# A hybrid decoder step: 44 instead of 60 adaLN weight pieces inside of the recurrence

## The chip, the cores and the metric

The kernel runs on one core of a Trainium2 chip. The metric is the device time of one execution in microseconds, the median of several runs. Beside the runs there is one profiled execution, from which all rows below come.

## The reference, cut to what matters

A trunk of two layers is computed for a prompt of 256 rows and for 8 single rows (264 columns in all), with d_model 2048 and d_ff 5632. Layer 0 mixes with RWKV-7, layer 1 with an RG-LRU; behind each mixer stands a ConvFFN. Each of the four blocks has its own shift, scale and gate, and they come from the condition `c` by one wide product for each layer:

```python
mod = (jax.nn.silu(c) @ P['w_mod'][i] + P['b_mod'][i]).reshape(B, N_MOD, 1, D_MODEL)
sh_m, sc_m, gt_m, sh_f, sc_f, gt_f = [mod[:, j] for j in range(N_MOD)]
h = rms_norm(x, P['norm_g'][i, 0]) * (1 + sc_m) + sh_m
...
out, shift_new, S = rwkv7_time_mix(...)
...
x = x + gt_m * rms_norm(out, P['norm_g'][i, 1])
```

So of the 12 vectors of `mod` the first two are needed at once, and the other ten only as the blocks are reached: the gate of the mixer behind the recurrence, the shift and scale of the first ConvFFN after that, and so on. `w_mod` is 2048 x 12288 for each layer in f32. The recurrence of RWKV-7 is, per head and step, S = S * d + (S a) b + v k and y = S r; the kernel works it out in chunks of 64 steps, for 16 pairs of heads.

## The kernel before

The program has four stages for layer 0: the projections (weights streamed in groups, each a matmul of three for hi and lo parts), the recurrence over 16 pairs of heads, the output projection, and the ConvFFN; then layer 1 with RG-LRU and ConvFFN. Everywhere but in the recurrence TensorE multiplies streamed weights: `Stream` (`ws`) loads raw tiles of 1 MB, two groups in each, ScalarE and VectorE split each group into `wh` (L434) and `wl` (L435), and 24 matmuls of 264 columns (L455 to L457) use it.

The ten later vectors of `mod` are cut into 160 pieces of 1 MB (`in_wmr`), 16 for each vector. A piece is loaded into a raw tile and used by 4 matmuls of 512 columns in `wm_mm` (L345); after 16 of them VectorE transposes the sum (L394) and `mod_fin` finishes the vector. There are two places for it:

- Inside of the recurrence, by `pump_load` (a step that issues the first half of the load, and a step for the second, L1397) and `pump_step` (the matmuls). The first `NPUMP` pieces go there.
- Behind it, by `mm_group`, which calls `wm_pump(1)` after every `PACE`-th group of weights; that uses the piece loaded before and loads the next (L375). `residual_and_h` puts in four more at each of three seams, and `mod(layer, vec)` forces in what a vector still lacks when it is asked for.

Raw tiles go around in a ring of `NRAW + stg["n"]`, five outside of the recurrence, where weights and pieces share it. In the recurrence `stg["n"]` is 0 and only the `NRAW` resident tiles `raw` are left, for pieces and four loads of the sample's low-rank weights:

```python
def raw_tile():
    i = stg["i"]
    stg["i"] = (i + 1) % (NRAW + stg["n"])
    return rawp([128, 2048], F32, "raw", NRAW) if i < NRAW else stg["p"](..., "rawx", stg["n"])
```

A tile that comes around again may be loaded only when its last reader is done, and the load's issue waits for that on SyncE, in order with all other transfers of the recurrence.

What runs when in the recurrence is written out by hand in the string `ORDER`. Each entry is a letter and a number, with a count ahead of it: `l` load, `p` prep, `d` diag, `s` solve, `v` levels, `b` prepb, `q` seq, `o` out (for the pair with that number), `a` a piece of the sample's state, `g`, `h`, `e` the sample's preparation, gate and end, `w` a step of the load of a piece, `u` its matmuls. Each entry runs its job to its next `yield`, and the instructions so issued are put on each engine in that order: a table that sets all five engines' queues.

Of the kernel before, what the change touches and what calls it, by code (L numbers as in the profile page):

```python
# [38 lines left out]
l3 w1 p2 d0 3p2 4p1 a1 2b0 d1 b0 2b1 3g0 3p2 b1 p2 l5 p2 3p3 l3 2p3 2b0 d0 d1 s0 p3 w1 2p3 u0 u1 2p2 s2 3p3
5b1 p4 p3 2l4 g0 2p4 p5 s0 2p5 p4 3g0 l5 p5 w2 s0 w2 w3 2g0 p2 w3 g0 l6 p2 d2 p3 g0 5p2 6p3 d3 u2 u3 2g0 s0  # L40
3p4 2b2 w4 p4 3p5 b2 b1 4p4 b1 2p5 2b2 g0 s0 3b2 d2 d3 w4 2s2 5g0 p5 w5 3g0 2p4 u4 3p4 l7 p4 3b3 p5 2s2 s0 p5
2b3 g0 2b2 w5 u5 3b3 g0 p5 2w6 2p5 p4 2p5 p6 q0 2p6 2a0 2p5 u6 2a0 2q0 l6 s0 v0 b3 p6 2a0 5p6 b3 p6 s2 a0 p6
a0 3v0 2p7 a0 4h0 l8 l9 p7 l7 p7 d5 d4 l8 w7 2h0 3p7 4p8 v1 p7 v1 h0 2v1 l9 2p7 2v0 h0 p7 2p9 h0 p9 v1 s2 v1
p9 3v0 2v1 v0 v1 d4 d5 v1 2a1 p7 v0 q0 p6 w7 u7 2w8 u8 3s4 2a1 3q0 s2 2v2 q0 v1 w10 v2 3q0 p7 a1 p7 3q0 p7 2w9
v2 p6 l10 2q0 2p6 q0 2p6 s4 q0 2p6 a1 3p7 v3 3q0 v3 a0 s4 2a1 w10 v2 2p8 q0 2o0 q0 v3 v2 3b4 p8 a1 u9 u10 a1
p7 2p8 d6 3p8 l10 a2 p10 v3 o0 3p10 b5 o0 a2 q1 v3 2q1 d7 q1 2w11 o0 d6 q1 v3 s4 2a2 v2 d7 s4 v2 a2 a3 v2 w12
q0 2o0 s6 2p8 d8 2q1 v2 2o0 p8 a2 s4 3q1 o0 v2 p8 p9 s6 q1 l12 2q1 2a2 d8 q1 v3 q1 2p8 2a2 2p9 v3 4o0 3v3 3v4
q1 v4 3b4 a3 a2 b4 p8 b4 p9 3a3 w12 u11 u12 p9 v4 b4 3q1 2v4 a4 v4 b4 4q1 3a3 v4 h0 2s6 2w13 3p9 2b5 2p10 2b5
p10 2w14 b6 a3 2l11 3b5 a3 2v4 p10 p11 q1 a4 u13 u14 a3 2w15 b5 2o1 2w16 s6 a5 b5 3p9 p10 2q2 2a4 p9 q2 p9 d9
v5 2o1 a4 o1 2p11 2p9 o1 2v5 o1 s6 p11 s6 2q2 o1 u15 3q2 2w17 a4 2o1 a4 b7 d9 s8 3q2 2v5 a4 v5 2q2 a4 3q2 u16  # L50
4q2 s6 2w18 v5 q2 b6 p11 2q2 2p11 3v5 p11 3o2 3v6 3p10 v5 o1 b6 2p12 u17 u18 q3 p12 q3 a4 l12 p12 v6 a5 3p10
2q3 2l13 2b6 q3 o1 a4 q3 2b6 2w19 v6 2o2 w20 v6 s8 q3 a5 q3 p10 2q3 b6 q2 2o2 2p10 a5 w20 2a5 3v6 a6 u19 u20
p10 l14 o2 4q3 4a5 d10 2o2 w21 4q3 2v6 a5 2b6 q3 w21 2q3 p12 b7 q3 2p12 b7 o3 o2 o3 q4 s8 u21 d10 2o1 w22 2o2
w22 w23 u22 q4 q3 4p11 3q4 o2 p11 2a6 2q4 3p11 b8 4q4 2p11 2v7 w23 u23 2w24 2v7 d11 p13 2v7 a7 3p13 q3 p11 2q4
u24 2w25 w26 5q4 p12 w26 3v7 4s8 3q4 2a6 d11 2o3 l14 2q4 o4 p12 2v7 o3 u25 2o4 p12 2q5 2p12 q4 3a6 p12 2q5 w27
s10 w27 2a6 p12 d12 2p12 2b8 s14 a7 3p13 p12 a7 s8 4p14 2o3 q5 o3 o4 p13 u26 u27 q5 2p12 o4 v8 2l15 2o3 3v8 o3
d12 3q5 2b7 a7 2b7 3q5 2b8 q5 2a7 b8 4q5 b7 2w28 u28 o4 2p14 w29 b7 o3 q5 2o4 a7 b7 v8 b8 w29 o4 v8 o4 u29 3b8
v8 2q5 o4 a6 2a7 2w30 2v8 2s10 2o3 q5 v8 2q5 p13 v9 o5 2w31 a7 3p13 u30 a8 a7 u31 v8 o5 o4 5b9 a8 q6 a8 q5
2p13 3q6 a8 q6 2p13 2s10 b10 s10 p13 2b9 3a8 2w32 u32 q6 p15 2p14 p15 p14 p15 2w33 3o5 q6 p15 2w34 s10 d13 2q6
2o4 q6 u33 q6 w35 2q6 w35 b9 a8 v9 3q6 v9 2p13 v9 q6 2a8 2b9 q6 d13 2q6 v9 o5 2q6 p15 v9 o6 2p15 q6 a9 p15 o6  # L60
u34 u35 q7 o5 a8 p14 q7 2o5 2w36 w37 2p14 3q7 2o5 s10 p14 a9 p14 d14 p14 w37 4q7 v9 u36 w38 2v9 3a9 q7 p15 2v9
2a9 4q7 2b10 3q7 s12 4b10 w38 4q7 s12 2p14 3a9 2q7 a9 v10 u37 u38 a10 v11 2s12 v10 2p15 s12 p15 b11 p15 2v10
2p15 2w39 2p15 a11 4b11 v10 2b11 2v11 v10 2a10 3v10 v11 q6 q7 u39 2o6 s12 2o7 q8 d15 v10 4q8 v10 2w40 u40 2w41
2q8 a10 o5 s12 2o6 a10 2o6 o5 u41 5q8 w42 o5 w42 o6 2q8 o6 q8 o7 o6 o7 q8 u42 o7 p14 w43 q8 a10 2q8 a10 w43
3a10 v11 3q8 o8 q8 w44 o6 w44 o8 q9 v11 2o6 o7 4q9 2o8 2o7 q9 2a11 p14 a11 q9 u43 u44 d14 d15 o7 s12 v12 2q9
w45 o7 q9 w45 o8 2w46 o8 v12 4q9 3o8 2q9 o7 u45 3q9 v12 2w47 v12 o8 2v12 4q9 2o9 2s14 q10 o7 a11 2o7 o9 q10
s14 2q10 a10 q8 q10 2o9 b10 u46 2o8 3o9 2w48 u47 q10 b10 o9 q10 o9 b10 2q10 2b12 2q10 b12 3b11 4o9 o8 u48 2q10
b12 2q10 o8 q10 2b12 2w49 q9 b12 2a11 b12 2a11 q10 b13 3q10 2w50 b13 2q10 2s14 q10 2b12 2o10 u49 u50 a12 o10
q10 2o10 6b13 2a11 b14 w51 2b14 w51 4b14 a12 o10 u51 4o10 v13 2w53 2b13 3v11 3v12 a12 b14 3a12 v13 2p15 2v13
a12 2v11 v12 w52 v13 w52 q11 v13 u52 u53 2q11 v12 3a12 3q11 2a13 2b14 q11 v13 q11 s14 q11 v13 b15 q11 s14 q11  # L70
2v14 v13 a12 2o10 v14 w54 v14 v13 4a13 v14 w54 a13 v13 v14 w55 q11 w55 q11 u54 5q11 o10 3a13 q11 a13 2q11 b15
2q11 o10 2o11 q12 u55 2o11 q12 b15 2q12 o11 b15 v15 2q12 b15 2q12 2a14 b15 q12 2b15 a14 q12 2o11 2v15 4q12 v15
2o11 2w56 a14 q12 o11 3q12 q11 2v15 2a14 2q12 2b15 2q12 2o12 a14 q13 2q12 u56 2o11 2o12 o11 a14 2o12 o11 3q13
3o12 2q13 w57 o12 2a14 2q13 3o12 2q13 v14 2q13 o12 v14 2q13 v15 v14 q13 w59 2v15 2v14 a15 q13 4a15 2q13 2a15
w57 u57 3q13 a15 3q13 2o13 q14 v15 3q14 a15 v15 5q14 a15 3q14 o13 e0 o13 a15 10q14 o14 e0 o14 q14 4q15 o13
4q15 w58 6q15 o14 q15 e0 q15 w58 6q15 u58 e0 2o13 q15 2e0 q14 o14 o15 o14 e0 w59 u59 o15 2o13 2o14 4o13 o14
o13 6o14 a14 q15
# [1714 lines left out]
```

## Time and profile before

| | us |
|---|---|
| median of 3 runs | 2910.57 |
| lowest, highest | 2909.17, 2916.7 |
| profiled execution | 2907.63 |
| its span | 2905.9 |
| TensorE busy (matmul) | 2786.0, 96% |
| VectorE, ScalarE, GpSimd busy | 1756.3, 1366.6, 511.6 |

The span runs from the first to the last instruction. The recurrence is the stretch from 397 to 772 us: its first matmul on L969 starts at 397.51, and the first matmul of the output projection at 770.86.

### The profile page before, as it was taken

Reading aid. Unit: us, or ns where it says so; the run is one execution under the profiler, and the core shown is the slowest. Engines: PE = TensorE matmul, PEld = TensorE weight load, DVE = VectorE, ACT = ScalarE, POOL = GpSimd, SP = SyncE. Lnnn points to the kernel's source line nnn. Section 1 sums busy time; section 2 is a strip of 40 time slices with the busy share of each in tenths; the row PEclk is TensorE's granted clock in tenths of the full one; section 3 lists DMA queues with packets and bytes.
Section 4 is the critical chain, followed back from the end, with each engine's and each line's share of the span. In section 5 each row is a group of like instructions: output and inputs, shape, how many; then the busy total and the mean of one; then the engine's idle time right before and its main releaser. Section 6 shows DMA issues by size and latency. Waiting matters only on the chain.

```text
span 2905.9 us, 61725 instructions
## 1 busy us (share of the span) xinstructions
PE 2786.0 (96%) x25868; PEld 2529.8 (87%) x25868; DVE 1756.3 (60%) x2830; ACT 1366.6 (47%) x2195; POOL 511.6 (18%) x1044
## 2 busy tenths in 40 slices
PE   7999988989899999999999999999999999999997
...
DMA  8777557887565666666666665566666645545452
GB/s 329 285 264 257 171 162 230 286 269 250 209 248 214 234 242 229 235 234 231 233 235 229 242 258 188 220 231 221 261 221 236 231 176 181 182 177 186 174 188 77
DMA packets 148438, 648.48 MB, mean 223 GB/s; under 512 B 41360, under 2 KB 60960, under 8 KB 81600
## 3 DMA queue, kind: packets, MB, share of 16 engines
...
q14 instruction: 76, 0.62, 0.1%
...
## 4 chain that ended last, share of the span: by engine, by line
PE 74%; DMA 4%; DVE 3%; ACT 2%; issue 1%; SPq 0%; POOL 0%; DVEq 0%; ACTq 0%; POOLq 0%
PE bk L455 16%; PE bk L456 15%; PE bk L457 15%; PE sq L455 6%; PE sq L456 6%; PE sq L457 6%; PE wm L345 5%; DMA raw<-in_wmr 3%; PE bk L895 1%; DVE bt L545 1%; ACT wh L434 0%; PE bk L901 0%; DVE U L546 0%; PE bk L582 0%; PE bk L1231 0%
## 5 line engine op out<-in xcount | busy, mean ns | idle before, releaser
L435 DVE TENSOR_TENSOR wl<-rawx,wh 128x1024 fp32r<-128x1024 f32 x460 | 565.4, 1231 | 488.2 <-ACT wh L434 468.5
L434 ACT CAST wh<-rawx 128x1024 fp32r<-128x1024 f32 x460 | 481.1, 1048 | 663.2 <-PE bk L456 454.2
L455 PE MATMUL bk<-AH,wh 128*128 128x264 f32 x2352 | 672.7, 286 | 0.0
L457 PE MATMUL bk<-AH,wl 128*128 128x264 f32 x2352 | 668.7, 284 | 0.2 <-DVE wl L435 0.2
L456 PE MATMUL bk<-AL,wh 128*128 128x264 f32 x2352 | 668.8, 284 | 0.0
L435 DVE TENSOR_TENSOR wl<-raw,wh 128x1024 fp32r<-128x1024 f32 x300 | 369.3, 1233 | 329.8 <-ACT wh L434 323.3
L455 PE MATMUL bk<-ah,wh 128*128 128x264 f32 x1822 | 525.7, 289 | 8.0 <-ACT ah L488 5.5
L457 PE MATMUL bk<-ah,wl 128*128 128x264 f32 x1822 | 520.8, 286 | 0.5 <-DVE wl L435 0.5
L456 PE MATMUL bk<-al,wh 128*128 128x264 f32 x1822 | 520.8, 286 | 0.0
L434 ACT CAST wh<-raw 128x1024 fp32r<-128x1024 f32 x300 | 313.7, 1048 | 434.8 <-PE bk L456 285.0
L455 PEld LDWEIGHTS bk<-AH,wh 128*128 128x128 f32 x2352 | 443.4, 189 | 34.4 <-issue 29.3
L456 PEld LDWEIGHTS bk<-AL,wh 128*128 128x128 f32 x2352 | 442.7, 188 | 0.2 <-DVE AL L489 0.2
L457 PEld LDWEIGHTS bk<-AH,wl 128*128 128x128 f32 x2352 | 441.8, 188 | 0.4 <-DVE wl L435 0.4
L455 PEld LDWEIGHTS bk<-ah,wh 128*128 128x128 f32 x1822 | 344.2, 189 | 33.9 <-issue 21.6
L457 PEld LDWEIGHTS bk<-ah,wl 128*128 128x128 f32 x1822 | 344.6, 189 | 1.4 <-DVE wl L435 0.8
L456 PEld LDWEIGHTS bk<-al,wh 128*128 128x128 f32 x1822 | 344.7, 189 | 0.6 <-DVE al L489 0.2
L455 PE MATMUL sq<-AH,wh 128*128 128x264 f32 x1040 | 297.3, 286 | 0.0
L456 PE MATMUL sq<-AL,wh 128*128 128x264 f32 x1040 | 295.7, 284 | 0.0
L457 PE MATMUL sq<-AH,wl 128*128 128x264 f32 x1040 | 295.4, 284 | 0.0
L1525 POOL COPY fgs<-gt 128x10 f32<-128x10 f32 x88 | 49.4, 585 | 1306.8 <-ACT gt L1519 1285.6
L455 PEld LDWEIGHTS sq<-AH,wh 128*128 128x128 f32 x1040 | 196.0, 189 | 15.2 <-issue 13.4
L456 PEld LDWEIGHTS sq<-AL,wh 128*128 128x128 f32 x1040 | 195.7, 188 | 0.0
...
## 6 DMA issues: line engine op xcount, KB each, us to landing
...
```

Source lines behind the costliest of these rows:

```text
L345: PE.matmul(ps[32 * g:32 * g + 32, :cols], cs[:, k0 + kk, :], raw[:, (kk * 4 + g) * cols:(kk * 4 + g + 1) * cols], start=(k0 + kk == 0), s ...
L434: S.copy(wh, t)
L435: V.tensor_sub(wl, t, wh.bitcast(F32))
L455: PE.matmul(ps[:, :n], h[:, kk, sl], xh, start=first and kk == 0, stop=False)
L456: PE.matmul(ps[:, :n], h[:, kk, sl], xl, start=False, stop=False)
L457: PE.matmul(ps[:, :n], l[:, kk, sl], xh, start=False, stop=last and kk == 1)
L545: e.tensor_tensor(t, U1[:, j:j + n, :TP], r1[:, None, :TP].to_broadcast([128, n, TP]), op=mult)
L895: PE.matmul(out[HH[(i + turn) % 2]], lhs[HH[i]], rhs[HH[i]], start=start, stop=stop, skip_group_check=True)
L1525: G.tensor_copy(gs[:, m], gt[:, TP:])
```

## The change

`NPUMP` falls from 60 to 44, so 116 instead of 100 pieces go behind the recurrence. `NRAW` rises from 2 to 3: three resident tiles go around in the recurrence, and outside the ring of five is three resident and two others. `PACE` falls from 5 to 4, so a piece goes with every fourth group of weights. `ORDER` is written anew; it holds the same steps of all other jobs. No function changes.

```diff
-PACE = 5
-NRAW = 2
+PACE = 4
+NRAW = 3
 CW = (3, 1)
-NPUMP = 60
+NPUMP = 44
...
 ORDER = """
-p0 s0 h0 g0 l0 p0 l0 3p0 g0 3p0 2l1 4p1 4p0 2g0 4p1 g0 3p1 p0 p1 b0 a0 4p0 l2 2p0 p2 b0 l2 2b0 2p1 w0 p1 b0 w0
...
+p0 p1 2g0 2l0 2p0 l1 p1 p0 s0 l1 p0 g0 3p0 l2 4p0 p1 l3 2p0 2w0 5p1 2p0 4p1 p2 3p0 p2 2g0 p3 p2 l2 p2 3p1 3b0
...
```

SyncE in the middle of the recurrence, before: `raw` from `in_wmr` is half a piece, `ss` and `sS` the sample's state; PE in the bracket is a wait for a matmul, the DMAHW names are waits for earlier transfers.

```order
L1397 DMA raw_7923<-in_wmr 128x1024 [waits DMAHW1_49,PE_49]
L1397 DMA raw_7923<-in_wmr 128x1024
L1397 DMA raw_7938<-in_wmr 128x1024 [waits PE_49]
L1397 DMA raw_7938<-in_wmr 128x1024 [waits DMAHW4_49]
L1358 DMA out_sS<-ss_7229 128x512 [waits DMAHW5_49]
L1397 DMA raw_8032<-in_wmr 128x1024 [waits DMAHW2_49,DMAHW6_49,DMAHW1_49,PE_49]
L1397 DMA raw_8032<-in_wmr 128x1024 [waits DMAHW7_49]
L1397 DMA raw_8079<-in_wmr 128x1024 [waits DMAHW3_49,DMAHW4_49,DMAHW0_49,PE_49]
L1397 DMA raw_8079<-in_wmr 128x1024
L1335 DMA ss_8093<-in_swkv 128x512 [waits DMAHW5_49]
L1358 DMA out_sS<-ss_7504 128x512 [waits DVE_49]
```

The same place now (`vj`, `kj` are a pair's values and keys, `lu2` its gate weights):

```order
L1396 DMA raw_7952<-in_wmr 128x1024 [waits DMAHW5_49,PE_49]
L1396 DMA raw_7952<-in_wmr 128x1024 [waits DMAHW6_49]
L1396 DMA raw_7989<-in_wmr 128x1024 [waits DMAHW7_49,PE_49]
L1396 DMA raw_7989<-in_wmr 128x1024 [waits DMAHW0_49]
L1334 DMA ss_8013<-in_swkv 128x512 [waits DMAHW1_49,DVE_49]
L1029 DMA vj_8075<-Vd_97 128x256 [waits DMAHW2_49,DVE_49]
L1396 DMA raw_8101<-in_wmr 128x1024 [waits DMAHW3_49,PE_49]
L1396 DMA raw_8101<-in_wmr 128x1024 [waits DMAHW4_49]
L956 DMA kj_8108<-Kd_96 128x256 [waits DMAHW5_49,Pool_49]
L1196 DMA lu2_8126<-in_lup 128x256 [waits DMAHW6_49,PE_49]
L1396 DMA raw_8160<-in_wmr 128x1024 [waits DMAHW7_49]
L1396 DMA raw_8160<-in_wmr 128x1024 [waits DMAHW0_49]
```

Before, five rows of pieces are broken by one other transfer and each piece's first row waits for a matmul; now two other transfers stand between them twice, and the last piece's first row waits for none.

SyncE at the end of the recurrence, before: `pS` is a pair's final state, `in_wst` the weights of the output projection.

```order
L1397 DMA raw_10582<-in_wmr 128x1024 [waits DMAHW6_49,DMAHW3_49,PE_49]
L1197 DMA lu2_10606<-in_lup 128x256 [waits DMAHW4_49]
L1397 DMA raw_10582<-in_wmr 128x1024
L1186 DMA out_pS<-St_10526 64x64 [waits DVE_49]
L1186 DMA out_pS<-St_10526 64x64 [waits DMAHW7_49]
L1397 DMA raw_10367<-in_wmr 128x1024 [waits DMAHW0_49]
L1358 DMA out_sS<-ss_10071 128x512 [waits DMAHW1_49]
L1186 DMA out_pS<-St_10627 64x64 [waits DMAHW2_49,DVE_49]
L1186 DMA out_pS<-St_10627 64x64 [waits DMAHW3_49]
L1197 DMA lu2_10728<-in_lup 128x256 [waits DMAHW4_49,PE_49]
L420 DMA raw_10753<-in_wst 128x2048 [waits DMAHW5_49]
L420 DMA raw_10755<-in_wst 128x2048 [waits DMAHW6_49,DMAHW0_49]
```

And now:

```order
L1258 DMA so2_10495<-sd2_5759 128x1x128
L1396 DMA raw_10462<-in_wmr 128x1024 [waits DMAHW3_49]
L1396 DMA raw_9971<-in_wmr 128x1024 [waits DMAHW4_49]
L1396 DMA raw_9674<-in_wmr 128x1024 [waits DMAHW5_49]
L1185 DMA out_pS<-St_10512 64x64 [waits DMAHW6_49,DVE_49]
L1185 DMA out_pS<-St_10512 64x64 [waits DMAHW7_49]
L1185 DMA out_pS<-St_10378 64x64 [waits DMAHW0_49]
L1185 DMA out_pS<-St_10378 64x64 [waits DMAHW1_49]
L1357 DMA out_sS<-ss_10016 128x512 [waits DMAHW2_49]
L1357 DMA out_sS<-ss_9824 128x512 [waits DMAHW3_49]
L1196 DMA lu2_10610<-in_lup 128x256 [waits DMAHW4_49,PE_49]
L419 DMA raw_10635<-in_wst 128x2048 [waits DMAHW5_49]
```

The last halves of the pieces moved ahead of the last two pairs' state transfers, where one stood behind them; the first weights follow the last `lu2` in both.

TensorE at the end of the recurrence, before: `yb` is the last state step's output, `wm` the pieces; the other rows are `pair_out` of the last pairs and the sample's transpose (`sy`).

```order
L895 MATMUL yb_10547<-E_10050,rb_10626 64x64 x2
L345 MATMUL wm_9408<-raw_10582,cT_72 32x512 x4
L1210 MATMUL bk_10648<-blk_108,gsq_10493 128x2 x2
L1390 MATMUL bk_10657<-ident_107,sy_5460 128x128
L1202 MATMUL bk_10663<-yh_10539,cen_113 128x256
L1203 MATMUL bk_10663<-yl_10540,cen_113 128x256
L345 MATMUL wm_9408<-raw_10367,cT_72 32x512 x4
L1219 MATMUL bk_10648<-ident_107,gsd_10651 64x128 x4
L1210 MATMUL bk_10683<-blk_108,gsq_10662 128x2 x2
L1231 MATMUL bk_10691<-lw_98,lu2_10485 128x256 x2
L1219 MATMUL bk_10683<-ident_107,gsd_10686 64x128 x4
```

And now:

```order
L1209 MATMUL bk_10526<-blk_108,gsq_10393 128x2 x2
L1201 MATMUL bk_10532<-yh_10404,cen_113 128x256
L1202 MATMUL bk_10532<-yl_10405,cen_113 128x256
L344 MATMUL wm_8646<-raw_10462,cT_72 32x512 x4
L344 MATMUL wm_8646<-raw_9971,cT_72 32x512 x4
L344 MATMUL wm_8646<-raw_9674,cT_72 32x512 x4
L1209 MATMUL bk_10557<-blk_108,gsq_10531 128x2 x2
L1218 MATMUL bk_10526<-ident_107,gsd_10555 64x128 x4
L1230 MATMUL bk_10571<-lw_98,lu2_10246 128x256 x2
L1218 MATMUL bk_10557<-ident_107,gsd_10565 64x128 x4
L1230 MATMUL bk_10582<-lw_98,lu2_10411 128x256 x2
```

Two pieces, four rows apart, became three in one row, behind the first norm matmuls of the last pairs instead of ahead of them.

## Rows read from the trace of the kernel before

**Rows 1.** The slices of the page: TensorE and the DMA engines.
```profile
PE   7999988989899999999999999999999999999997
...
DMA  8777557887565666666666665566666645545452
```

**Rows 2.** Busy time by stage: recurrence in three stretches and whole, then behind it.
```profile
core 0: us, PE busy (x) PEld busy (x) DVE busy (x) ACT busy (x) POOL busy (x), PEclk, DMA share, GB/s
397.00:547.00 150.00, 123.93 (x2271) 79.38 (x2270) 106.54 (x257) 78.96 (x189) 74.08 (x175) 0.94 0.81 250
547.00:697.00 150.00, 133.03 (x2405) 79.28 (x2397) 82.46 (x186) 62.32 (x173) 64.48 (x163) 0.98 0.85 271
697.00:772.00 75.00, 62.48 (x1241) 41.70 (x1239) 42.08 (x103) 30.72 (x93) 11.44 (x14) 0.80 0.52 174
397.00:772.00 375.00, 319.44 (x5900) 200.35 (x5898) 231.08 (x545) 172.00 (x455) 149.99 (x351) 0.93 0.77 244
1000.00:1050.00 50.00, 50.00 (x409) 46.63 (x402) 26.88 (x36) 20.77 (x28) 3.13 (x12) 1.00 0.62 229
2400.00:2450.00 50.00, 50.00 (x413) 50.00 (x413) 28.02 (x39) 22.32 (x30) 4.17 (x12) 1.00 0.48 179
```

**Rows 3.** The same view, adaLN pieces (L345) alone, over the recurrence.
```profile
core 0: us, PE busy (x) PEld busy (x), PEclk, DMA share, GB/s
397.00:772.00 375.00, 94.42 (x480) 14.52 (x480) 0.93 0.77 244
```

**Rows 4.** Waits over the recurrence: in total, times, longest (us).
```profile
PE wm L345 <- DMA raw<-in_wmr: 24.4, 20, 4.3
...
PEld wm L345 <- DMA raw<-in_wmr: 54.5, 40, 5.2
```

**Rows 5.** The waits of TensorE, middle stretch, 547 to 697 us.
```profile
PE wm L345 <- DMA raw<-in_wmr: 15.7, 15, 4.3
```

**Rows 6.** Chain of work over the recurrence: shares by line, and one long piece.
```profile
by line: DMA raw<-in_wmr 24.8%; PE wm L345 12.1%; PE bk L895 6.1%; PE bk L901 3.7%; issue 3.5%; PE bk L1231 2.3%; PE bk L1219 2.2%; PE sq L895 2.1%; PE bk L914 2.0%; PE yb L895 1.9%; DMA xc<-sx 1.6%; PE bk L1210 1.5%; DMA ss<-in_swkv 1.5%; 
...
637.57 8.88 DMA raw<-in_wmr
```

**Rows 7.** TensorE in order of time: a split piece, later a whole one.
```profile
551.04 1.05 PE L345 MATMUL wm<-raw,cT 128*32 128x512 f32 x4
553.61 1.05 PE L345 MATMUL wm<-raw,cT 128*32 128x512 f32 x4 [1.52 <-DMA raw<-in_wmr]
...
726.28 1.07 PE L345 MATMUL wm<-raw,cT 128*32 128x512 f32 x8
```

**Rows 8.** SyncE in order of time, middle stretch: loads and the next transfer.
```profile
548.15 6.88 SPq L1397 DMA_DIRECT2D raw<-in_wmr  x3
555.08 0.43 SPq L1030 DMA_DIRECT2D vj<-Vd  x1
```

**Rows 9.** TensorE in order of time, the recurrence's last two pieces.
```profile
754.98 1.93 PE L345 MATMUL wm<-raw,cT 128*32 128x512 f32 x8
...
758.53 1.94 PE L345 MATMUL wm<-raw,cT 128*32 128x512 f32 x8
```

**Rows 10.** TensorE in order of time, first ConvFFN: two pieces.
```profile
983.64 1.06 PE L345 MATMUL wm<-rawx,cT 128*32 128x512 f32 x8
...
999.43 1.07 PE L345 MATMUL wm<-raw,cT 128*32 128x512 f32 x8
```

**Rows 11.** Chain of work, seam before the second ConvFFN (start, us, what).
```profile
2076.03 2.71 PE wm L345 x24
```

More of the change, by code (lines that the diff above doesn't have):

```diff
@@ L37 @@
 ORDER = """
-p0 s0 h0 g0 l0 p0 l0 3p0 g0 3p0 2l1 4p1 4p0 2g0 4p1 g0 3p1 p0 p1 b0 a0 4p0 l2 2p0 p2 b0 l2 2b0 2p1 w0 p1 b0 w0
[L39 to L77, printed above, removed]
+p0 p1 2g0 2l0 2p0 l1 p1 p0 s0 l1 p0 g0 3p0 l2 4p0 p1 l3 2p0 2w0 5p1 2p0 4p1 p2 3p0 p2 2g0 p3 p2 l2 p2 3p1 3b0
@@ new lines @@
+p2 b1 p2 b0 2w1 b0 3p2 4p1 g0 b0 l3 l4 d1 p3 p2 l4 d0 b0 p2 2p3 2b1 w2 3b0 u0 w2 2p3 2p2 2p3 p4 p3 5p2 3p3 2p4
+a0 d0 g0 d1 p4 2g0 b2 p2 u1 3b1 2s0 p3 h0 p3 2g0 d2 2l5 2p3 u2 d3 b1 p5 2w3 s0 d2 g0 s0 4g0 w4 g0 2s0 d3 2p4
+2b1 2p3 b1 2p4 4b2 s2 p4 l6 p4 p3 2g0 2p4 w5 2p5 s2 4p5 3g0 4p4 b3 2p4 g0 2p5 u3 3p5 2g0 3b2 b3 p5 2b3 s0 p5
+g0 p5 b3 2p5 v0 3p6 2v0 w4 2v0 u4 l6 v1 q0 g0 p6 s2 2g0 a0 l7 p4 v0 p5 w6 v1 p5 s2 3a0 2s2 l7 2p6 a0 p6 2q0
+3p7 b2 2v1 w5 u5 2p7 b2 2p6 w6 u6 v0 p6 p7 2p6 2v1 2v0 2b3 2v0 4a0 b3 3h0 2b3 l8 b4 4p7 l8 h0 s2 p8 p7 s4 d5
@@ new lines @@
+2p8 h0 2q0 v1 d4 p8 q0 p9 v1 q0 l9 w7 s2 v2 3p7 4h0 2q0 3v1 q0 d4 3q0 l9 2q0 2p9 a1 p7 d5 2q0 p7 s6 p7 p9 6p6
+2p7 2q0 a1 2q0 b5 3v2 2q0 d7 2o0 l10 w8 b4 p6 v3 b4 q1 p8 l11 2v2 2q1 w8 q1 v3 2s4 3p8 2v2 v3 a1 w7 s4 q1 2p8
+v2 u7 o0 2s4 q1 v3 3q1 v2 q1 d6 2p8 q1 p9 w10 a0 v2 v3 o0 v3 a1 2w9 w10 2a1 2p9 3q1 s4 q1 3a1 2p8 l10 2q1 d6
+d7 3o0 s6 q1 o0 a1 u8 u9 2p10 p9 p8 2o0 2p10 3a2 u10 2b4 2a2 b4 a1 3q1 s4 v4 v3 b4 2v3 3a2 2q1 v5 p9 3v4 2v3
+2p8 3b5 2b4 2b5 p8 2p9 a2 p9 w12 2o0 v4 b5 b4 2w11 w12 b5 u11 u12 v4 s6 2b5 o0 2o1 l11 6q2 v4 q0 2w13 u13 o0
@@ new lines @@
+2v4 2a2 p8 s6 2v5 o1 3a3 2w15 2v4 w14 p9 v5 3q2 2p9 2q2 a3 2p9 a3 d8 p9 2s6 3q2 p10 p11 q2 w14 2o1 2p11 p10
+2q2 p9 q2 2v5 2p10 w16 2a3 3q2 o1 s10 d8 q2 s6 2a3 p11 q2 o2 2o1 u14 u15 o1 o2 p10 w16 2p10 q3 p10 v5 3q3 o2
+u16 2v5 a4 v5 p12 o1 v5 s6 v6 b6 2o2 q1 v6 d9 2q3 p11 a3 q3 2a4 b6 a3 p10 3q3 l12 v6 w17 a4 q2 2a4 v6 b6 q3 a4
+2b6 3q3 w17 4p10 a4 o1 b6 q3 v6 2b6 p10 l12 3q3 v6 q3 p11 s8 q3 b6 2q3 o3 2a4 o3 a5 q3 a5 w18 p10 w18 b6 2p12
+2o2 u17 b7 o2 l13 3q4 b7 p11 3p12 d9 2q4 w19 u18 b7 w19 d10 2o2 5p11 2w20 l13 a5 4q4 2v6 3v7 p12 v7 v6 a5 o2
@@ new lines @@
+q4 a4 2s8 p12 2p11 v6 o1 2q4 u19 v6 p12 2o1 o2 s8 2w21 d11 2q4 2p11 a6 3q4 2v7 2p11 w22 p11 q4 w22 3q4 p13 3a5
+p13 2o2 p13 2q4 u20 2l14 2p13 u21 o3 p13 o3 2p12 o4 v7 2p12 o4 o3 q5 a5 o4 p14 2a5 2s8 v7 a6 2v7 2w23 q3 s8
+2p12 4q5 p13 v7 p12 p14 p12 w24 3a6 o3 a6 2p14 a6 w24 3q5 o4 u22 u23 2q5 2o3 q5 2o3 s8 3o4 2q5 b8 3q5 v8 o3
+2b7 2o4 b7 q5 o4 q5 v8 2p12 2b7 a6 q5 2v8 a5 2b8 q5 b8 a6 o3 q5 d10 q4 l15 2p13 3b8 2b7 2v8 2q5 u24 d11 s10
+3b8 2w25 2o5 v8 q6 2w26 2s10 2q6 a6 2a7 v8 u25 v8 2q6 v9 2p14 p13 2v8 a7 3q6 2a7 o4 b9 2o3 q6 a7 2b9 a7 3q6
@@ new lines @@
+2w27 2o4 l15 u26 o4 p13 u27 s10 3o5 p15 2b9 3p13 w28 q6 w28 w29 2q6 s10 3p13 w29 a7 3q6 a6 b9 s10 q6 q5 q6 2b9
+q6 p14 3v9 2q6 3p15 b9 2o5 w30 u28 2p13 b9 3o6 u29 q7 v9 b10 q7 2o5 w30 p14 o5 s14 v9 b10 2a7 b10 3p14 d12 3q7
+3v9 o6 s12 u30 v9 a8 p14 p15 s10 2q7 v9 2q7 p15 o6 p14 p15 q7 2b10 2a8 w31 v10 w31 3q7 2p14 q7 d13 b10 2q7 v10
+2a8 2q7 u31 2w32 q7 p14 2v10 b10 2q7 3a8 2p15 a7 q7 2o7 q7 a8 q8 p14 2v10 q6 u32 4q8 v10 2o5 v11 q8 v10 2o5
+2v10 d12 d13 s12 2w33 q7 v10 q8 p15 a8 p15 2q8 b11 p15 5b11 q8 o6 a8 b11 2o7 3q8 3a9 q8 u33 3o6 2w34 q8 p14 o7
```

13 lines of the change are left out of this document (added).

## The prediction

> **What bounds the kernel now.** I read the slices of the page first, to find where TensorE is not the limit, then the busy time of each stage, then the waits inside of the one stage that has some, and last the chain of work through it.
>
> The slices [rows 1] show a TensorE at 9 tenths or more almost everywhere, with 8s among them in slices 6 to 11 of 40: that is the recurrence, and in slices 7 to 10 the DMA engines are at 7 or 8 tenths, more than anywhere later. By stage [rows 2]: the recurrence lies from 397 to 772 us, 375 us long. TensorE is busy for 319.4 of them and idle for 55.6. Behind it TensorE has no idle time at all: 50.00 of 50 us. So time saved in the recurrence is time saved, and work put behind it costs its full length.
>
> What the adaLN pieces do in the recurrence is in [rows 3]. A piece is 8 rows of the trace (4 matmuls, each shown twice), and 480 rows are 60 pieces. They are busy for 94.4 us, 1.57 each, though a piece whose data is there takes 1.07 from start to end, some 1.0 beside its neighbours [rows 7]. The difference is the wait: each half of a piece has its own load, and where the second half is late, the piece falls apart into two runs of 1.05 us with a hole of 1.52 between them [rows 7]. TensorE's idle time before such halves is 24.4 us in 20 waits, most of it in the wait of 15.7 us that the middle stretch shows; its weight loads wait for the same transfers another 54.5 us, partly under a matmul that still runs [rows 4, 5]. The chain of work says the same: the loads of pieces are the largest part of it, 24.8% of the 375 us, one of them 8.88 us [rows 6].
>
> Why they are late: two tiles hold the pieces, so a load starts only when the piece two before it is done, and SyncE stands at that load with all other transfers queued behind it (three loads in a row take it 6.88 us [rows 8]). The transfers themselves have room: 244 GB/s over the stage against 271 in its middle stretch [rows 2].
>
> **The change, part by part.** The sum is made against the profiled execution, 2907.6 us with a span of 2905.9; it lies 2.9 under the median of the runs, 2910.6.
>
> 1. 16 pieces leave the recurrence. In flow 1.0 us each: -16.0.
>
> 2. The third tile. A load may now start when the piece three before it is done, and pieces stand further apart (44 in the stage for 60). Two terms can shrink: the stretch of the pieces, 94.4 - 60 x 1.0 = 34.4 us, and the idle time, 24.4 us. Bounds: nothing of it goes, or all 58.8. I take two thirds per piece, since a free issue takes SyncE 0.43 us and three loads took 6.88 [rows 8]: most of that delay is the wait to be issued, which a third tile takes away, while a load issued in time still needs some us to land. What is left: (34.4 + 24.4) / 3 x 44 / 60 = 14.4. Gain: -44.4.
>
> 3. What is late next. In the middle stretch TensorE's idle time is 16.97 us, and 15.7 of it are these loads: only 1.3 us in 150 go to other engines. The two other stretches idle 26.07 and 12.52, of which at most 24.4 - 15.7 = 8.7 are loads: about 30 us in 225, or 0.133 per us, go to VectorE, ScalarE and small transfers [rows 2, 4, 5]. With the loads out of the way the middle stretch will wait for those as the others do: bounds 0 and the whole gain of parts 1 and 2, 60 us; I take the rate of the nearest stretches, 0.133 x 115 = +15.
>
> 4. The new order of the steps. Its parts are the same instructions, so it has a price only in waits, which part 3 has. Two places can be read from the rows of the order. In the middle, SyncE had four pieces' loads with one other transfer among them, each first half waiting for TensorE; now two pieces, two other transfers, a piece, two others and a piece follow each other, and the last one's first half waits for no matmul any more. At the end, TensorE had one piece right behind the last state step and one four rows later; now three stand in a row. A piece there takes 1.93 us, with a granted clock of 0.80 in that stretch (part of it at the lower of the two levels, 1.2 GHz) [rows 2, 9]: one more is +1.9. Their loads stand ahead of the last two pairs' state transfers on SyncE, so I don't charge a wait; if one came it would cost at most a load as long as the longest, 8.88 [rows 6]. The first weights behind the recurrence are queued behind the last gate load in both versions: 0.
>
> So the recurrence goes from 375 to 375 - 16.0 - 44.4 + 15 + 1.9 = 331.5 us.
>
> 5. The pieces that come back later. 116 instead of 100 are left, and one goes with every fourth group of weights instead of every fifth. Counting groups (24 in the first output projection, 256 in a ConvFFN, 56 and 32 in the RG-LRU) pieces go 6 for 4, 64 for 52, 14 for 11 and 8 for 6: 19 more inside of full TensorE. By then 144 pieces are done, as many as the second ConvFFN's scale needs; before it was 141, and three pieces were forced in at that seam. Price in full TensorE: two pieces are 15.79 us apart [rows 10]; five groups without a piece take 5 x 24 x 50 / 413 = 14.53 [rows 2]; a piece is 1.26. 19 x 1.26 = +23.9. The seam gives back the three pieces that the chain shows there, 2.71 [rows 11]. Net +21.2. The transfers have room for it: three tiles of 1.05 MB, two of weights and a piece, in 4 x 2.906 + 1.26 = 12.9 us are 244 GB/s, under the 271 of [rows 2], so 0 for them; bound from above, if each of the 116 waited for its load as the 60 do now, 24.4 / 60 x 116 = 47, of which I take nothing, since the 50 us with pieces of [rows 2] have no idle time.
>
> Sum: -16.0 - 44.4 + 15 + 1.9 + 21.2 = -22.3. 2907.6 - 22.3 = 2885.3; against the median 2888.3. I say **2888**.
>
> **A rule that speaks against the change.** The weight loads are busy for 200.35 of 375 us in the recurrence, 53%, and for 46.6 of 50 behind it [rows 2]. The Trainium skill (Perfetto Trace Analysis, Identifying the Most-Contended Engine) says to judge TensorE's headroom by the busy share of its weight loads and not of its matmuls, and (Optimization Strategy) that stages with different most-contended engines may gain by being interleaved. By that rule the recurrence has the free room for pieces, and moving them behind it puts them where there is none: parts 1 and 2 would be nothing and the sum +23. Against it, in this trace, stand the 24.4 us in which TensorE waits for pieces and nothing else, so I follow the rows and keep the rule's outcome as the third rival.
>
> **Rivals.**
>
> First, all of the waiting goes. Parts 1 and 2 in full are -16 - 58.8 = -74.8, part 3 is 0: -74.8 + 1.9 + 21.2 = -51.7, or 2859. For it: only 1.3 us of other idle time in the middle stretch. Against it: VectorE is busy for 106.5 of 150 us in the first one, which a faster TensorE makes denser.
>
> Second, the wait stays with each piece: the third tile doesn't help, because SyncE still comes to the load late, behind a transfer whose data isn't ready. Then 16 pieces take their share along, 16.0 + 16 x 58.8 / 60 = 31.7; part 3 shrinks in proportion to 15 x 32 / 60 = 8. Sum -31.7 + 8 + 1.9 + 21.2 = -0.6: 2910, no change. That is also what a change that doesn't do what it says would give: fewer pieces, no third tile in effect.
>
> Third, slower: the recurrence doesn't wait for loads at bottom but for the chain of small dependent steps (state update, copy, matmul), and each load that arrives earlier uncovers one of these. Its place is the middle stretch, its price that parts 1 to 3 cancel: 1.9 + 21.2 = +23, 2934. It decides from the point where the recurrence shortens by less than 21.2 - 8.7 = 12.5 us. For it: of the 38.6 us of idle time outside of the middle stretch at most 8.7 are loads. Against it: in the middle one 15.7 of 16.97 are.
>
> **Chances.** The measurement tells a change from none at about 0.3%, 8.7 us: 2902 to 2919 counts as the same. The forecast (2871 to 2902) 0.53, the first rival (under 2871) 0.20, the second 0.14, the third 0.13. Faster is the forecast and the first rival, 0.73; same 0.14; slower 0.13. For eight in ten I leave out the slower case and the far end of the first rival (more than all of the waiting gone, by an order that packs better): 2853 to 2909.
>
> **What would show it.** Part 1 and 2: a recurrence of about 330 us with 352 rows of pieces, busy for under 60 us, and TensorE's idle time for their loads at some 6 us for 24.4. Part 3: more waits for VectorE and ScalarE in the middle. Part 4: three pieces in a row at the end, 1.9 us each, without a hole. Part 5: pieces 12.9 us apart behind the recurrence, TensorE still full, and no three pieces at the seam near 2076 us; everything from the first output projection on 21 us longer. Wrong I am if the recurrence keeps more than 360 us, if its idle time moves to other releasers in the same size, or if a piece in full TensorE costs much more than 1.26 us.

## The result, and the profile after

The changed kernel takes 2886.47 us (median of 4 runs, 2882.78 to 2888.66) against 2910.88 for the kernel before on the same chip: a ratio of 0.9911, with an interval of 0.9894 to 0.9929. It is faster by 24.4 us; 2888 was forecast. Its profiled execution is 2882.8 us with a span of 2881.0, 24.9 under the span of before.

Where it came from can be read from three ends. The first matmul of the recurrence's decay (L968, L969 before) starts at 399.93 us, 2.4 later than before; the first matmul of the output projection at 726.25, 44.6 earlier; and from there to the end of the span it is 2154.8 us for 2135.0. So the recurrence itself went from 373.35 to 326.32 us (-47.0), and the stages behind it became 19.7 us longer. 2.4 - 47.0 + 19.7 = -24.9.

The view of [rows 2], busy time by stage, of the changed kernel (the columns are the stretch, its length, each engine's busy time and instructions, then the granted clock, the DMA engines' share and GB/s):

```profile
397.00:547.00 150.00, 121.78 (x2284) 82.40 (x2285) 108.15 (x256) 79.82 (x194) 67.28 (x167) 0.91 0.79 244
547.00:672.00 125.00, 118.50 (x2561) 82.07 (x2561) 89.34 (x198) 65.43 (x185) 75.82 (x173) 1.00 0.80 251
397.00:727.00 330.00, 286.29 (x5772) 196.95 (x5771) 231.82 (x541) 169.98 (x455) 152.21 (x351) 0.93 0.73 228
1000.00:1050.00 50.00, 50.00 (x404) 46.07 (x403) 23.25 (x29) 21.56 (x30) 2.09 (x6) 1.00 0.69 252
```

The last row is the first ConvFFN: as full as before, though a piece comes with every fourth group now. In the recurrence, the middle stretch has 6.5 us of idle TensorE in 125; before it had 17 in 150. The pieces alone, as in [rows 3], and the waits, as in [rows 4]:

```profile
397.00:727.00 330.00, 55.14 (x352) 10.17 (x352) 0.93 0.73 228
```

```profile
PE bk L1247 <- DMA raw<-in_lups: 5.3, 1, 5.3
PE bk L454 <- ACT wh L433: 4.6, 1, 4.6
PE bk L968 <- DMA lu<-in_lup: 4.4, 2, 2.2
PE bk L894 <- DVE St L1177: 4.2, 8, 2.2
...
PE wm L344 <- DMA raw<-in_wmr: 3.0, 1, 3.0
PEld wm L344 <- DMA raw<-in_wmr: 6.5, 6, 3.9
```

44 pieces are busy for 55.14 us, 1.25 each for 1.57 before; TensorE waits for their loads 3.0 us for 24.4, its weight loads 6.5 for 54.5. The chain of work over the stage, as in [rows 6], has the loads at 3.9% instead of 24.8%, and no line of it stands out:

```profile
by line: issue 9.5%; PE wm L344 7.1%; PE bk L894 4.8%; DVE smt L929 4.5%; POOL xs L1083 4.2%; DMA raw<-in_wmr 3.9%; POOL xtmp L1081 3.8%; DMA rawx<-in_wst 3.4%; PE bk L900 3.0%; DMA xc<-sx 2.8%; PE sq L894 2.7%; DVE cum L986 2.3%; PE bk L11
```

The end of the recurrence ([rows 9]) and two pieces behind it ([rows 10]), TensorE in order of time:

```profile
712.33 5.02 PE L344 MATMUL wm<-raw,cT 128*32 128x512 f32 x24
717.28 0.61 PE L1209 MATMUL bk<-blk,gsq 128*128 128x2 f32 x4
...
726.25 0.59 PE L454 MATMUL bk<-ah,wh 128*128 128x264 f32 x1 [4.61 <-ACT wh L433]
...
899.63 1.06 PE L344 MATMUL wm<-raw,cT 128*32 128x512 f32 x8
912.51 1.06 PE L344 MATMUL wm<-rawx,cT 128*32 128x512 f32 x8
```

Three pieces in a row without a hole, and pieces 12.88 us apart, just 4 x 2.906 + 1.26. All of it looks like the forecast come true. What made it, the profile of the change doesn't say: fewer pieces, a third tile and a new order came together.

### The profile page after: what moved, and what is told of

Read it like the earlier page. It is cut to its first block, busy times and chain, and to the rows that moved or that the text cites. A ratio compares the mean times of both kernels' runs of the same rounds, so it can differ in the third digit from the quotient of the medians.

```text
span 2881.0 us, 61698 instructions
## 1 busy us (share of the span) xinstructions
PE 2770.9 (96%) x25868; PEld 2526.0 (88%) x25868; DVE 1761.3 (61%) x2830; ACT 1363.7 (47%) x2193; POOL 519.0 (18%) x1044
## 4 chain that ended last, share of the span: by engine, by line
PE 73%; DVE 5%; ACT 2%; POOL 2%; issue 2%; DMA 2%; SPq 0%; DVEq 0%; POOLq 0%; ACTq 0%
PE bk L454 16%; PE bk L455 15%; PE bk L456 15%; PE sq L454 6%; PE sq L455 6%; PE sq L456 6%; PE wm L344 4%; PE bk L894 1%; DVE bt L544 1%; DVE smt L929 1%; POOL xs L1083 0%; DVE wl L434 0%; DMA raw<-in_wmr 0%; POOL xtmp L1081 0%; DVE U L545 0%
## 5 line engine op out<-in xcount | busy, mean ns | idle before, releaser
L434 DVE TENSOR_TENSOR wl<-raw,wh 128x1024 fp32r<-128x1024 f32 x454 | 560.0, 1235 | 517.5 <-ACT wh L433 489.0
L433 ACT CAST wh<-raw 128x1024 fp32r<-128x1024 f32 x454 | 474.7, 1048 | 662.6 <-PE bk L455 448.7
L434 DVE TENSOR_TENSOR wl<-rawx,wh 128x1024 fp32r<-128x1024 f32 x306 | 376.3, 1231 | 319.5 <-ACT wh L433 299.2
L433 ACT CAST wh<-rawx 128x1024 fp32r<-128x1024 f32 x306 | 320.4, 1048 | 461.4 <-PE bk L455 336.2
L454 PEld LDWEIGHTS sq<-AH,wh 128*128 128x128 f32 x1040 | 196.0, 188 | 19.7 <-issue 16.8
```

The source lines that it names most:

```text
L433: S.copy(wh, t)
L434: V.tensor_sub(wl, t, wh.bitcast(F32))
L454: PE.matmul(ps[:, :n], h[:, kk, sl], xh, start=first and kk == 0, stop=False)
```

## The experiments

"Recurrence" is the time from the first decay matmul to the first matmul of the output projection; the ratio is against the kernel before on the same chip. Old and new order mean the table `ORDER` of before and after.

| run | order | pieces, tiles | recurrence, us | median, us | ratio (interval) |
|---|---|---|---|---|---|
| before | old | 60, 2 | 373.35 | 2910.88 | |
| e1 | old | 60, 3 | 366.75 | 2905.48 | 0.9986 (0.9977 to 0.9996) |
| e2 | old | 44, 2 | 359.99 | 2916.80 | 1.0025 (1.0010 to 1.0040) |
| e3 | old | 44, 3 | 361.71 | 2919.76 | 1.0031 (1.0015 to 1.0047) |
| after | new | 44, 3 | 326.32 | 2886.47 | 0.9911 (0.9894 to 0.9929) |
| e4 | new | 0 | 321.67 | 2972.20 (one run) | |
| e5 | old | 0 | 339.94 | 2988.74 (one run) | |
| e7 | old | 60 without loads | 325.28 | 2861.80 | 0.9819 (0.9796 to 0.9841) |
| f44 | new, last pieces earlier | 44, 3 | 326.82 | 2888.00 | 0.9925 (0.9909 to 0.9942) |
| e6 | f44's, loads moved | 44, 2 | 353.92 | 2909.46 | 0.9997 (0.9984 to 1.0009) |
| g44d | as e6 | 44, 3 | 339.88 | 2896.86 | 0.9963 (0.9950 to 0.9975) |
| g52 | f44's, 8 added | 52, 3 | 351.42 | 2899.86 | 0.9964 (0.9951 to 0.9977) |
| f60 | f44's, 16 added, 6 loads moved | 60, 3 | 367.29 | 2907.31 | 0.9992 (0.9980 to 1.0005) |
| g60 | new, evenly | 60, 3 | 373.05 | 2915.87 | 1.0027 (1.0016 to 1.0039) |

**The parts apart.** Theory A is the forecast: the waits for the loads are time of the stage, and the third tile, with 16 pieces fewer, takes most of them. Its rival E gives the gain to the new order of the steps.

*e1: the third tile alone.*

```diff
-NRAW = 2
+NRAW = 3
```

> The kernel before with three resident tiles instead of two; its 60 pieces, its order and every fifth group stay. Theory A (a load is late because its issue waits for a tile): two thirds of the 58.8 us that pieces wait go, some 13 us of other waits come, the recurrence goes from 373 us to about 347, the time to about 2885. Theory B (SyncE comes to the load late for other reasons, a tile more doesn't help): the waits for piece loads stay near 24 us of TensorE's idle time, 2906 to 2914. Theory C (the chain of small steps sets the stage): the waits for loads go, others of the same size come, 2906 to 2914.

The recurrence is 6.6 us shorter, and the time 0.14% lower. Of the three theories B is nearest, but the waits for loads did fall, by less than a third. The tile did what it was to do on SyncE. Its two longest waits at the pieces' loads, over the recurrence, before and then in this run:

```profile
SPq L1397 <- DMA raw<-in_wmr: 37.5, 22, 5.3
SPq L1397 <- PE wm L345: 19.6, 19, 1.9
```

```profile
SPq L1397 <- PE wm L345: 5.4, 9, 1.1
SPq L1397 <- DMA raw<-in_wmr: 5.3, 8, 1.2
```

SyncE's rows of the stretch of [rows 8], and the waits of TensorE and its weight loads over the recurrence, in this run:

```profile
548.19 1.39 SPq L1397 DMA_DIRECT2D raw<-in_wmr  x3
550.62 0.54 SPq L1030 DMA_DIRECT2D vj<-Vd  x1
```

```profile
PE wm L345 <- DMA raw<-in_wmr: 18.7, 16, 3.3
PEld wm L345 <- DMA raw<-in_wmr: 37.1, 26, 4.2
```

The three loads in a row take SyncE 1.39 us for 6.88, and the transfer behind them goes out at 550.62 instead of 555.08. The third of them goes out 5.5 us earlier (549.16 for 554.70). But the row begins at 548.19, and at 548.15 before: the same place. A free tile lets a load go out when the table comes to it, and no earlier. Matched load by load in the two traces, a piece's second half is issued a median of 8.3 us ahead of its matmuls, and 7.3 before; half a piece takes a median of 6.0 us to land (before):

```profile
raw<-in_wmr SPq DMA_DIRECT2D x120, 512.0 KB, 6.0
```

So TensorE still waits for them 18.7 us of 24.4.

*e2 and e3: 44 pieces in the old order, with two tiles and with three.* 16 pieces and their loads are taken out of the table evenly; all other steps stay.

```diff
-PACE = 5
+PACE = 4
-NPUMP = 60
+NPUMP = 44
 # e3 also: NRAW = 3
 # ORDER: 16 of the 60 u, evenly, removed with both of their w; the rest renumbered
```

> The kernel before with 16 of its 60 pieces taken out of its own order, evenly, two tiles as before, every fourth group behind. Theory A: the wait for each piece stays with two tiles, so the recurrence gives 16 + 15.7 us less 8 of other waits, 349 us, and 20 us come back behind: 2905 to 2911. Rival D (pieces further apart do it, not the tile): the recurrence falls to some 330 us and the time to about 2888.

> All of the change but its new order: the order of before with 16 of 60 pieces taken out evenly, three tiles, every fourth group. Theory A (the order itself is worth little): recurrence 325 to 335 us, time 2882 to 2892, as the changed kernel. Rival E (the new order brings the gain): recurrence over 345 us, time over 2900.

Both are slower than before: the recurrence gives 13.4 and 11.6 us, and the pieces cost 20 to 22 behind it. e2 meets neither of its expectations (360 us of recurrence, where 349 and 330 were expected). With 44 pieces in the old order, the third tile brings nothing (359.99 and 361.71). e3 is the whole change but for the order of the steps. It still has most of the wait, and a lower granted clock than before (0.89 for 0.93). Busy time over the recurrence, the pieces' share of it, and the wait:

```profile
397.00:760.00 363.00, 304.45 (x5775) 205.91 (x5775) 227.97 (x542) 170.82 (x455) 150.31 (x352) 0.89 0.66 206
```

```profile
397.00:760.00 363.00, 67.65 (x352) 10.27 (x352) 0.89 0.66 206
```

```profile
PE wm L345 <- DMA raw<-in_wmr: 16.0, 14, 3.5
```

So rival E holds and the forecast's step 2 falls as an account: from e3 to the changed kernel only the table differs (the places of steps, pieces and loads), and that takes 35.4 us out of the recurrence. TensorE's rows say where. From e3's 363 us to the changed kernel's 330, pieces are busy 12.5 us less (67.65 to 55.14), waits for their loads are 13.0 less (16.0 to 3.0), other matmuls 5.7 (236.80 to 231.15) and other idle time 1.9 (42.6 to 40.7): 25.5 of the 33 us stand at the pieces.

**Is it a shorter chain of steps, or pieces better placed?**

*e4 and e5: no pieces in the recurrence*, in the new and in the old order. What they lack is computed behind it in heaps, so only the recurrence is read.

```diff
-NPUMP = 44          # e5: 60
+NPUMP = 0
 # ORDER: all u and w removed (e5 with NRAW = 3, PACE = 4)
```

> The changed kernel with none of the 44 pieces in the recurrence (they are all worked off behind it, with stops there, so only the recurrence's length is read). Theory A: 44 pieces cost the recurrence about what TensorE is busy with them, 55 us, and some 5 us of waits, so it falls from 328 us to 265 to 285. Theory C (chain of small steps): it stays over 305, since the pieces ride in gaps.

> The order of before with no pieces in the recurrence (all 160 go behind it or before its end is needed, so only the recurrence is read: from the first L969-type matmul near 398 us to the first output-projection matmul; it was 772 with 60 pieces, 757 to 760 with 44). Theory C, the chain of small steps in the old order is the longer one: it ends near 745 to 760, about as with 44 pieces, and 25 us or more after the new order without pieces (720.96). Theory P, the old order's chain is as short as the new one's and it only places its pieces badly: the 0.7 to 0.8 us that each of the 16 removed pieces gave go on, 44 more give 31 to 37 us, and it ends near 720 to 728.

The new order without pieces takes 321.67 us, only 4.65 less than with 44, as theory C had it. The old one takes 339.94, between the two expectations for it. Read alone, that says that the old order has the longer chain, and that the waits lay in its shadow. The busy time of the two shows what else was taken away (as before: PE, PEld, DVE, ACT, POOL, clock, DMA, GB/s; e4 first, then e5):

```profile
397.00:721.00 324.00, 267.65 (x5415) 213.17 (x5413) 224.08 (x535) 168.73 (x455) 150.94 (x351) 0.82 0.33 89
```

```profile
397.00:737.00 340.00, 269.49 (x5416) 215.66 (x5414) 230.75 (x535) 169.65 (x454) 152.40 (x352) 0.80 0.31 83
```

The changed kernel's other matmuls are busy for 286.29 - 55.14 = 231.15 us; the same matmuls take 267.65 in e4. Without pieces the granted clock fell from 0.93 to 0.82. So these two runs aren't "the stage less the pieces": they took away the work and, with it, part of the clock. Of the 18.3 us between e4 and e5, whose clocks are nearly the same, 14.2 are idle time of TensorE (56.4 and 70.5). A run was needed that leaves the pieces' matmuls where they are.

*e7: the kernel before without the pieces' loads.* Each of the 60 pieces multiplies a resident tile instead, so that their part of the modulation is not computed.

```diff
-        raw = wm_raw[i] = raw_tile()
+        wm_raw[i] = None                      # and no SP.dma_start for it
...
-                          raw[:, (kk * 4 + g) * cols:(kk * 4 + g + 1) * cols],
+                          csr if raw is None else raw[:, ...],    # csr: cs, 512 columns
```

> The kernel before, with 60 pieces at their places in the recurrence, but their 120 loads left out: each piece multiplies a resident tile of 512 columns, so that 60 pieces' contribution to the modulation is not computed; TensorE's work is the same. Step 2 of the forecast (the loads' waits of 58.8 us are time of the stage): the recurrence falls from 373 to 315 to 330 us, total 2850 to 2868. Theory C (the waits lie in the shadow of the old order's chain of small steps): 355 to 368, total 2892 to 2906. Between them, the loads are worth what is found: 1 us of the stage per us of it.

The recurrence falls to 325.28 us, 48.1 less, with all 60 pieces' matmuls and in the old order. Its busy time, the pieces' share of it, and its end:

```profile
397.00:725.00 328.00, 291.88 (x5914) 198.97 (x5914) 235.32 (x546) 170.40 (x455) 154.49 (x351) 0.93 0.31 86
```

```profile
397.00:725.00 328.00, 65.04 (x480) 11.41 (x480) 0.93 0.31 86
```

```profile
724.68 0.59 PE L455 MATMUL bk<-ah,wh 128*128 128x264 f32 x1 [2.36 <-ACT wh L434]
```

So the forecast had the worth of the waits right (58.8 less 15 given back is 43.8; 48.1 measured), and the theory that they lie in the shadow of a longer chain falls: with its pieces' matmuls in place and without their loads, the old order is as short as the new one. At a clock of 0.93 its other matmuls are busy for 226.84 us, 42.7 less than at 0.80 in e5. Against before, TensorE's pieces are busy 29.4 us less (94.42 to 65.04) and no longer wait for loads (24.4), 53.8 in all; other matmuls and other idle time give 6.7 back (225.02 to 226.84, 31.2 to 36.1). The DMA engines' share fell too, from 0.77 to 0.31, and SyncE has 120 loads fewer to issue, so 48.1 us is what the loads cost with all that they hold up, not the pieces' own wait alone.

What was slow is the old order with its loads. The new one reaches the same length with the loads of 44 pieces in place. The new order with its pieces' matmuls and without their loads was not run. So it is open whether its other steps are shorter too, which the 14.2 us of idle time between e4 and e5 would fit.

**What of the order does it?**

*f44: the last three pieces earlier.* In the changed kernel they stand in a row at the end; here they stand at three places among the last pairs' steps, and the loads of four other pieces go out later.

```diff
-... e0 5q15 w41 o13 q15 o14 o15 w42 u41 u42 w43 u43 o14 ...
+... 2w41 3q11 ... u41 o11 ... 2w42 3q12 ... u42 o11 ... 2w43 o12 ... u43 2q14 ...
```

> The new order, with the last three pieces (three in a row behind the last state step) moved to three places among the steps of the last three pairs, 30 to 130 steps earlier, each one loaded in one go. If pieces ride free wherever the chain leaves room: the 5.02 us of the three in a row at the end go, and nothing else comes: 2881 to 2884 for 2886.5. If the last pairs have no room either, the same time as the changed kernel, 2886 to 2888.

No difference (326.82 us), as the second expectation had it: the 5 us at the end are paid at other places. It serves as the base of the next ones.

*e6 and g44d: loads moved, with two and three tiles.* In f44's order, loads of ten pieces that stood, whole or in part, ahead of the piece two before are put behind it, by up to 30 steps, so that two tiles can do (19 halves are moved, most of them to a later place). e6 has two tiles, g44d the same table with three.

```diff
 # e6 and g44d against f44, three of the places in ORDER
-2b1 w2 3b0 u0 w2 2p3 2p2 2p3
+2b1 3b0 u0 2p3 2p2 2w2 2p3
-2w9 w10 ... u8 u9
+2w9 ... u8 2w10 u9
-2p10 w16 ... u14 u15 ... w16
+2p10 ... u14 2w16 u15
```

> The same as the kernel with the last three pieces earlier, but with two tiles: a load that stood ahead of the piece two before it is put right behind that piece; all other steps keep their places. Theory A (the third tile takes two thirds of the waits): the recurrence is 25 to 40 us longer, 2908 to 2925. Theory C (the order of the steps sets the length, loads wait in its shadow): at most 10 us longer, 2884 to 2894. Pairs of pieces that stand close together must wait for a whole load between them, some 6 us each for about 10 such pairs; where all of that shows it is 60 us.

> The run with the new order and two tiles, word for word the same order (its moved loads too), with three tiles again; the recurrence was 353.9 us with two tiles, and 326.8 with three tiles and the loads at their old places. If the number of tiles is what made that run slow: 326 to 332, total 2885 to 2892. If the places of the loads did it (they stand later, right behind the piece that frees the tile of two, and arrive late): 345 to 356, total 2903 to 2911.

By its time e6 bears theory A out (27.1 us longer, 2909), but g44d shows that half of that is the loads' places: it lies between its two expectations. With the steps, the pieces and the tiles of f44, the moved loads alone cost 13.1 us (326.82 to 339.88). With the same table, the third tile is worth 14.0 us (353.92 to 339.88); by the ratios of whole runs it is 11 and 10 us. So order and tile need each other. With 44 pieces, the new order with two tiles gives 6.1 us (e2 to e6), the tile in the old order nothing (e2 to e3), and both together 33.2 (e2 to f44). The waits for the loads in f44, g44d and e6, in this order:

```profile
PE wm L344 <- DMA raw<-in_wmr: 2.0, 4, 0.9
PEld wm L344 <- DMA raw<-in_wmr: 6.5, 8, 1.8
```

```profile
PE wm L344 <- DMA raw<-in_wmr: 9.3, 10, 3.7
PEld wm L344 <- DMA raw<-in_wmr: 18.2, 13, 4.6
```

```profile
PE wm L344 <- DMA raw<-in_wmr: 14.3, 14, 5.7
PEld wm L344 <- DMA raw<-in_wmr: 28.5, 21, 6.6
...
SPq L1396 <- PE wm L344: 42.8, 15, 5.9
```

Where loads come late, TensorE waits for them; where, besides, no tile is free, SyncE stands too (42.8 us in e6; 12.5 in g44d and 10.6 in f44).

*f60, g52 and g60: more pieces in the new order.* If 44 pieces cost the recurrence 4.65 us, more of them should bring more.

```diff
-NPUMP = 44
+NPUMP = 60          # g52: 52
 # f60: 16 more in the widest gaps, loads of six others moved, three of them as in e6
 # g52: 8 more, six of them in the last third, one other load moved by 4 steps
 # g60: all 60 evenly, each load 30 table entries ahead
```

> The new order with 60 pieces instead of 44 in the recurrence: 16 more in the widest gaps between pieces, three tiles, still every fourth group behind. Behind it 16 pieces fewer at 1.26 us: -20. Theory C (pieces ride nearly free in the new order, 0.12 us each by the run without pieces): recurrence +2 to +5, total 2863 to 2870. Theory A of the forecast (a piece costs its 1.0 us in flow and a share of waits): recurrence +16 to +30, total 2882 to 2896. Rates of the old order (0.7 to 0.84 us a piece): recurrence +11 to +13, total 2874 to 2879.

> The kernel with the last three pieces earlier, and eight more pieces, most of them late in the stage, where the DMA engines are at 0.41 to 0.47, at places where SyncE comes to no load before its tile is free and no other load is moved. Theory S (the 40 us that 16 more cost came from loads at which SyncE stood, with the small transfers of the chain behind it; pieces themselves ride nearly free): recurrence +1 to +4, behind -10, total 2879 to 2883. Theory N (44 is about what the stage holds; each further piece costs 1.0 to 2.5 us wherever it is): recurrence +8 to +20, total 2886 to 2898.

> The new order with 60 pieces evenly spread over it, each load 30 steps ahead of its piece, so that with three tiles SyncE seldom stands at a load. Theory S: SyncE's time at these loads falls from 48 us (run with 16 more) to under 25 and the recurrence from 367 to 330 to 345, total 2868 to 2885. Theory N: it stays at 355 to 370, total 2895 to 2910, though SyncE stands less.

They don't. Eight more make the recurrence 24.6 us longer, 16 more 40.5, 60 spread evenly 46.2: 2.5 to 3.1 us for each piece beyond 44, and all that the new order had brought is gone with 60. All three are longer than any of their expectations allowed (+30, +20 and 370 us). In f60 a part of it can be the moved loads. Busy time over the recurrence and the pieces' share of it, in f44 and then in f60, and f60's wait of SyncE at the loads for the pieces ahead:

```profile
397.00:729.00 332.00, 287.63 (x5792) 200.63 (x5791) 232.51 (x542) 168.76 (x454) 153.35 (x351) 0.94 0.72 225
```

```profile
397.00:729.00 332.00, 52.40 (x352) 8.99 (x352) 0.94 0.72 225
```

```profile
397.00:769.00 372.00, 312.70 (x5918) 205.70 (x5916) 230.73 (x545) 169.62 (x454) 151.71 (x351) 0.91 0.77 246
```

```profile
397.00:769.00 372.00, 76.22 (x480) 11.76 (x480) 0.91 0.77 246
```

```profile
SPq L1396 <- PE wm L344: 26.9, 12, 4.1
```

Against f44, pieces are busy 23.8 us longer (76.22 for 52.40), other matmuls about the same (236.48 for 235.23), and TensorE is idle 14.9 us longer. In g52 and g60 SyncE stands 22.8 and 26.1 us at the same wait (the 48 us in g60's expectation are f60's three longest waits of SyncE at these loads). Theory S had wanted that under control and failed to get it, so its test is not a clean one. TensorE's own wait for the loads is not what makes these runs long: g52 shows none, and g60, where every load stands at least 35 steps ahead, shows little. Its busy time, the pieces' share of it, and that wait:

```profile
397.00:773.00 376.00, 314.98 (x5901) 205.90 (x5899) 230.48 (x544) 170.75 (x454) 149.40 (x351) 0.90 0.76 244
```

```profile
397.00:773.00 376.00, 73.37 (x480) 10.55 (x480) 0.90 0.76 244
```

```profile
PE wm L344 <- DMA raw<-in_wmr: 1.6, 3, 1.1
```

The recurrence is as long as before (373.05 and 373.35), where that wait was 24.4 us; now TensorE is idle for 59.4 us for other reasons, 31.2 before. What holds those other steps up, SyncE at the loads, the transfers' own time or the lower clock, stays open. Theory N is the nearest, with costs above its ranges. No kernel that computes all beat the changed one.

## Why the prediction was right, and where it was not

The time came out at 2886.5 for 2888. Step by step:

- **Step 5, the pieces behind**: forecast +21.2, measured +19.7, pieces 12.88 us apart, TensorE full, and no three pieces at the seam in the chain of work. Right.
- **Steps 1 to 4 together**, the recurrence: forecast 375 to 331.5, a loss of 43.5; measured 47.0. Right as a sum. By TensorE's rows the terms came true as well: pieces and the waits for their loads went from 94.42 + 24.4 to 55.14 + 3.0 us, -60.7 for -60.4 in steps 1 and 2, and the rest grew by 15.6 (other idle time 9.5, other matmuls 6.1) for 15 in step 3. What is wrong is which part of the change does it.
- **Step 2, the third tile, is the step that failed.** Priced at -44.4, it is worth -6.6 by itself with 60 pieces (e1) and nothing with 44 in the old order (e2 to e3), and the tile and the 16 pieces of step 1 together are worth -11.6 (e3), for -45.4 forecast in steps 1 to 3. The size of what could be won was right (48.1 us in e7); the lever was not. The reason given was that a load's delay is mostly its wait to be issued. That wait went (57.1 to 10.7 us in SyncE's two longest waits at these loads), and the loads still went out only 1.0 us (second halves) to 1.9 us (first halves) further ahead of their matmuls, since their places in the table are fixed. A tile gives leave to load earlier; someone has to use it.
- **Step 4, the new order**, was priced at +1.9 because its instructions are the same. With three tiles it took 35.4 us, with two 6.1 (e2 to e6). What step 2 booked for the tile is for the greater part this: the order moves the loads ahead, and the tile lets it. Counted in the two tables, the second half of a load stands a median of 14 steps ahead of its piece before and 31 after (of 1587 steps); the first half 23 and 42. In time it is issued 8.1 us ahead of its matmuls in e3 and 10.7 in the changed kernel. (In the middle of the recurrence, the rows of the order before are eight of four pieces, not five, with one other transfer among them.) That the places of loads alone are worth 13.1 us in one case, and a third tile 14.0, is shown by g44d and e6. How the 35.4 us divide between earlier loads and the places of the other steps is not; 25.5 of 33 us by TensorE's rows stand at the pieces. The first weights behind the recurrence, priced at 0, cost 2.2 (TensorE waits 4.61 for 2.45).
- **Step 3, what is late next**: +15 forecast. TensorE's idle time other than for pieces rose from 55.6 - 24.4 = 31.2 to 43.7 - 3.0 = 40.7 us, +9.5. In the middle stretch, where the forecast put all of it, it rose from 1.3 to 6.5, in the first one from 17.4 to 25.2, and in the last it fell from 12.5 to 9.0. With the 6.1 us of other matmuls the size is right, the place only in part.
- **The rivals.** The second one (the loads come late all the same, because of their place on SyncE) is nearest to what the change does without the new order: 2919.8, where it had said 2910. The third one's mechanism, waits in the shadow of the small steps, falls with e7 for the kernel before; g60 shows that with 60 pieces in the new order other waits do take the place of those for loads. That the order could be the gain was none of the rivals. The rule from the Trainium skill (Perfetto Trace Analysis, Optimization Strategy), that stages with different most-contended engines may gain by being interleaved, bears out as far as it goes: 44 pieces cost the new recurrence 4.65 us. How many fit, the busy share of the weight loads doesn't tell: it is 60% with 44 pieces (200.63 of 332 us in f44), and 58% with 52, which cost 24.6 us more.

A forecast of a change in three parts can be right by two errors that cancel, and here it was: that the time came out is in part luck. It took e3, the change without one part, to see it.
